# Reordering the projections of a hybrid encoder's even layer on one core: spatial value groups ahead of the heads' output gates

## The chip, the cores and the metric

The kernel runs on one core of one Trainium2 chip. The metric is the device time of one execution in microseconds (us), less is better. The core has five engines with instruction queues of their own, each worked off in order: TensorE (PE, with its weight loads shown apart as PEld), VectorE (DVE), ScalarE (ACT), GpSimd (POOL) and SyncE (SP, which issues most of the transfers).

## The reference, cut to what matters

Two layers over 1024 tokens of width 1024, float32. The change lies in the even layer's mixer:

```python
p = rms_norm(x) @ w_in                       # 24 blocks of 128 columns, plus 16 gate columns
qk, va, oa, gates, uv = split(p)             # q: blocks 0-3, k: 4-7, v: 8-11, oa: 12-15, u: 16-19, vb: 20-23
qk = silu(centred_dwconv(qk, conv_w))        # 5 taps
ha = rms_norm(h_fwd + h_bwd, head_g) * sigmoid(oa)      # 4 heads of a chunkwise mLSTM, both directions
u, vb = split(gelu(uv)); vb = rms_norm(vb)   # 4 groups
hb = u * (ws @ vb + bs)                      # in chunks of 128 tokens
x = x + concat([ha, hb]) @ w_out
```

After it come a squared-ReLU MLP, an attention layer, a second MLP and a final norm, none of which the change touches.

## The kernel before

Every weight block of 128x1024 is loaded on SP's queue (`raw`), rounded on ACT (line 411, `whi`) and its rest taken on POOL (line 412, `wlo`). A projection multiplies it with the normalized input in three passes (hi x hi, hi x lo, lo x hi): 48 matmuls of 128x512 into a PSUM tile `mm` of which there are two (line 432). DVE scales it on its way out of PSUM into a tile `pt` (`evac`, line 990). `AB_ORDER` is the order in which the blocks are loaded; the calls of `k_unit`, `q_unit`, `v_unit`, `o_unit`, `vb_unit` and `u_unit` must come in the same order.

What follows a projection:

- `k_unit`, `q_unit`: the convolution (ACT line 997, four DVE operations of line 1001, ACT Silu line 1003).
- `v_unit`, then `v_turn`: eight transposes of v (tile `vT`, line 1029) and two ACT copies.
- `o_unit`: an ACT Sigmoid (line 1036).
- `vb_unit`: an ACT Gelu (line 1047). `turn(g)` calls `sgu_values`: eight transposes (`vbT`, line 1424), ACT copies to `vn` (line 1426), and `tok_norm`. `mix(g)` calls `sgu_mix`: eight small products with `ws` (tile `sp`, line 1439, 16 matmul records) and two DVE operations (line 1440).
- `u_unit`: an ACT Gelu (line 1057) and a product with the group's `sp` on POOL (on DVE for the last group, line 1059).

Each head is a generator (`mlstm`), advanced by `step(h)`. Its five parts are: (1) the scores S (line 1277), the transposes kT (line 1286), their weighting on DVE, the decay matrices Dm from DRAM, masked on POOL and put through Exp on ACT; (2) the chunk states U (line 1304), with a chain of DVE operations (line 1313); (3) the products `int` and `intra` (lines 1339 and 1350), their sum, division (lines 1362 to 1371) and the sum of both directions on POOL (line 1385); (4) `tok_norm`; (5) eight transposes `hT` (line 1396) and two DVE products with the sigmoid of the output gate (line 1399).

`tok_norm` is an ACT square, a DVE reduction (line 1411), a chain of twelve DVE operations on 128x8 elements (lines 1413 and 477 to 486), each of which waits for the one before it, and a full-size product (line 1415).

All the small PE work takes its PSUM from one pool:

```python
pp = st.enter_context(tc.tile_pool(name="pab", bufs=4, space=PSUM, reuse_waits="tile"))
def sm(name="sm"):
    return pp.tile([P, 512], F32, tag="sm", name=self.uid(name))
```

SBUF tiles come from a ring of 45 slots, handed out in the order in which they were given back. In this stage no order is written out by hand: a planner lays the instructions of each engine out with priorities by the order of the program and estimated times, and hands its slots and tiles out in that order; the result is a fixed in-order list per engine. After `u_unit(3)` come the output projections (`mlp_inputs`, line 885), which read the eight tiles split by `add` (ACT line 501, POOL or DVE line 502), and the first MLP.

Of the kernel before, what the change touches and what calls it, by code (L numbers as in the profile page):

```python
# [76 lines left out]

AB_ORDER = (4, 0, 8, 5, 1, 9, 12, 6, 2, 10, 13, 7, 3, 11, 14, 15, 20, 21, 22, 23, 16, 17, 18, 19)  # L80

C_ORDER = (0, 1, 5, 2, 3, 4)

# [226 lines left out]
class Kern:  # L310
# [55 lines left out]
    def plan(self):  # L366
        A = self.A
        self.sd = [[self.dp.tile([4, P, 1024], F32, name=f"sd{i}_{j}") for j in range(NKP)] for i in range(2)]
        w = [(A["w_g"], NK * 48, True)]
        w += [(A["w_in"][i], 1024) for i in AB_ORDER]  # L370
        w += [(A["ab_out"][m], 1024) for m in MO]
# [572 lines left out]
    def ab(self, xh, xl, ss, spill):  # L944
# [37 lines left out]
        def evac(ps):  # L982
            t = self.slot(name="pt")
            with self.tc.high_priority():
                if isinstance(ps, list):
                    for h in range(2):
                        hs = slice(h * 512, (h + 1) * 512)
                        nc.vector.tensor_tensor(out=t[:, hs], in0=ps[h], in1=rb[:, hs], op=ALU.mult)
                else:
                    nc.vector.tensor_tensor(out=t, in0=ps, in1=rb, op=ALU.mult)  # L990
            return t
# [19 lines left out]
        def k_unit(h, ps=None):  # L1011
            R[h]["k"] = conv(4 + h, ps)

        def q_unit(h, ps=None):
            R[h]["q"] = conv(h, ps)

        def v_unit(h):
            R[h]["vt"] = evac(self.proj(xh, xl))

        def v_turn(h):  # L1020
            vt = R[h].pop("vt")
            v = R[h]["v"] = self.slot(F32, (P, NC, 130), "v")
            nc.gpsimd.memset(v[:, :, P:P + 1], 1.0)
            nc.gpsimd.memset(v[:, :, P + 1:P + 2], 0.0)
            for g in range(2):
                ps = sm("vT")
                for j in range(4):
                    c = 4 * g + j
                    nc.tensor.transpose(ps[:, j * P:(j + 1) * P], vt[:, c * P:(c + 1) * P], self.ident)
                with self.tc.high_priority():  # L1030
                    nc.scalar.copy(out=v[:, 4 * g:4 * g + 4, :P], in_=ps.rearrange("p (j e) -> p j e", e=P))
            self.drop(vt)

        def o_unit(h):
            oa = evac(self.proj(xh, xl))
            nc.scalar.activation(oa, oa, AF.Sigmoid)
            R[h]["oa"] = oa
# [3 lines left out]
        def vb_unit(g):  # L1041
            if g == 0:
                sg["ws"] = self.slot(name="ws")
                nc.sync.dma_start(out=sg["ws"][:, :512], in_=A["wsT"])
                nc.sync.dma_start(out=sg["ws"][:, 512:1024], in_=A["bs"].partition_broadcast(P))
            vb = evac(self.proj(xh, xl))
            nc.scalar.activation(vb, vb, AF.Gelu_apprx_tanh)
            sg[g] = vb

        def turn(g):  # L1050
            sg[g] = self.sgu_values(sg[g])

        def u_unit(g):
            u = evac(self.proj(xh, xl))
            if g == 3:
                self.drop(*xh, *xl)
            nc.scalar.activation(u, u, AF.Gelu_apprx_tanh)
            sp = sg.pop(g)
            (nc.vector if g == 3 else nc.gpsimd).tensor_tensor(out=sp, in0=sp, in1=u, op=ALU.mult)
            self.drop(u)  # L1060
            return sp

        def mix(g):
            sg[g] = self.sgu_mix(g, sg[g], sg["ws"][:, :512], sg["ws"][:, 512:])

        def step(h):
            next(G[h], None)
# [5 lines left out]
        for h in range(AH - 1):  # L1073
            k_unit(h + 1)
            if h > 0:
                step(h - 1)
            v_turn(h)
            step(h)
            q_unit(h + 1)
            step(h)  # L1080
            v_unit(h + 1)
            step(h)
            o_unit(h)
            step(h)
        o_unit(3)
        step(2)
        v_turn(3)
        step(3)
        vb_unit(0)
        step(3)  # L1090
        vb_unit(1)
        step(3)
        turn(0)
        vb_unit(2)
        step(3)
        turn(1)
        mix(0)
        vb_unit(3)
        step(3)
        turn(2)  # L1100
        mix(1)
        self.rope_tables()
        ah, al = [], []

        def add(t, **kw):
            hi, lo = self.split(t, **kw)
            ah.append(hi)
            al.append(lo)
            self.drop(t)
        late = []  # L1110
        for g in range(4):
            late.append(u_unit(g))
            if g == 0:
                turn(3)
                mix(2)
            if g == 1:
                mix(3)
                for h in range(AH):
                    add(R[h]["out"], pool=True)
            if g > 1:  # L1120
                add(late[g - 2], pool=True)
# [810 lines left out]
```

## Time and profile before

| | us |
|---|---|
| median of three runs | 2484.16 (2482.21 to 2487.2) |
| the profiled execution, its own time | 2484.26 |
| its span, first to last instruction | 2482.6 |

The span is 1.66 us shorter than the execution's own time. A time slice of the profile gives busy time of each engine in it; PEclk is the granted clock of TensorE as a share of 2.4 GHz. "idle before <-X" is the time for which the engine stood still ahead of an instruction, and whose end let it go.

### The profile page before, as it was taken

How to read it: one execution, taken by the hardware profiler on the slowest of the kernel's cores; microseconds unless marked ns; L12 is line 12 of the kernel's file. 1: busy time of each engine (PE TensorE's matmuls, PEld its weight loads, DVE VectorE, ACT ScalarE, POOL GpSimd, SP SyncE). 2: the span in 40 equal slices, each digit the busy share in tenths (PEclk: the TensorE clock that was granted, in tenths of full speed). 3: DMA queues.
4: the chain of work that ended last, by engine and by line, in shares of the span. 5: the costliest groups of instructions: out<-in, count | busy, mean ns of one | idle time of the engine just before them, and what ended most of it. 6: DMA issues, size and time to landing. Idle time of an engine off the chain costs nothing.

```text
span 2482.6 us, 31418 instructions
## 1 busy us (share of the span) xinstructions
PE 2405.1 (97%) x11947; PEld 1999.9 (81%) x11947; DVE 1773.4 (71%) x2504; ACT 1159.5 (47%) x1717; POOL 576.3 (23%) x362
## 2 busy tenths in 40 slices
PE   7999989999999999999999999998999999999997
PEld 5788877778887788887788888887878888788887
DVE  6765487777777676664788888887577777667665
ACT  3354444433333333353567677677443333333353
POOL 4233344200000000024545454546310000000023
PEclk9999999999999999999999999999999999999999
DMA  3211113365568634351000000002346655953432
GB/s 116 69 60 63 49 48 115 139 229 203 217 221 298 213 110 153 108 172 39 22 18 22 18 19 17 13 26 94 119 146 235 226 207 215 341 162 97 160 109 96
DMA packets 96631, 309.49 MB, mean 125 GB/s; under 512 B 9984, under 2 KB 12992, under 8 KB 96480
## 3 DMA queue, kind: packets, MB, share of 16 engines
q1 hardware_dynamic: 95296, 304.81, 35.1%
q10 hardware_dynamic: 1152, 2.62, 0.3%
q8 instruction: 94, 1.54, 0.3%
q14 instruction: 57, 0.47, 0.1%
q0 software_dynamic: 32, 0.05, 0.0%
HBM read 219.53 MB, written 87.92 MB: 124 GB/s over the span
## 4 chain that ended last, share of the span: by engine, by line
PE 87%; DVE 7%; DMA 3%; ACT 1%; issue 1%; POOL 1%; DVEq 0%; ACTq 0%; POOLq 0%; SPq 0%
PE mm L432 18%; PE y L792 11%; PE z L792 11%; PE A L655 7%; PE C L655 6%; PE D L655 6%; PE s L1680 6%; PE po L1733 4%; PE pt L1714 4%; PE pj L432 4%; PE B L655 3%; DMA raw<-w 1%; DVE mx L1684 1%; DMA hq<-hd 1%; DVE nm L1686 1%
## 5 line engine op out<-in xcount | busy, mean ns | idle before, releaser
L411 ACT CAST whi<-raw 128x1024 fp32r<-128x1024 f32 x163 | 169.2, 1038 | 453.1 <-issue 226.5
L412 DVE TENSOR_TENSOR wlo<-raw,whi 128x1024 fp32r<-128x1024 f32 x110 | 138.6, 1260 | 208.9 <-ACT whi L411 204.8
L432 PE MATMUL mm<-hi,wlo 128*128 128x512 f32 x680 | 218.1, 399 | 2.6 <-POOL wlo L412 2.5
L432 PE MATMUL mm<-hi,whi 128*128 128x512 f32 x680 | 218.4, 399 | 0.0
L432 PE MATMUL mm<-lo,whi 128*128 128x512 f32 x680 | 218.3, 399 | 0.0
L1699 POOL TENSOR_SCALAR pr<-pr,rs 128x1024 f32<-128x1024 f32 x128 | 144.4, 1128 | 242.7 <-DVE rs L1698 203.2
L655 PE MATMUL A<-xo,wo 128*128 128x512 f32 x768 | 190.8, 397 | 1.4 <-DVE x L885 1.4
L655 PE MATMUL D<-xo,wo 128*128 128x512 f32 x768 | 188.8, 394 | 0.0
L1684 DVE TENSOR_REDUCE mx<-s 128x1 f32<-128x1024 f32 x128 | 155.6, 1216 | 46.5 <-PE s L1680 45.8
L655 PE MATMUL C<-xo,wo 128*128 128x512 f32 x768 | 188.6, 394 | 0.0
L412 POOL TENSOR_TENSOR wlo<-raw,whi 128x1024 fp32r<-128x1024 f32 (+1 forms) x53 | 131.2, 2477 | 244.4 <-ACT whi L411 208.1
L792 PE MATMUL y<-hi,wlo 128*128 128x512 f32 (+1 forms) x464 | 180.7, 389 | 2.5 <-DVE wlo L412 2.5
L792 PE MATMUL y<-hi,whi 128*128 128x512 f32 (+1 forms) x464 | 180.8, 390 | 0.0
L1692 ACT ACTIVATE pr<-s,nm,rqs 128x1024 f32<-128x1024 f32 x128 | 154.7, 1209 | 55.1 <-DVE nm L1686 53.2
L792 PE MATMUL y<-lo,whi 128*128 128x512 f32 (+1 forms) x464 | 180.3, 389 | 0.0
L655 PEld LDWEIGHTS A<-xo,wo 128*128 128x128 f32 x768 | 146.1, 191 | 35.5 <-issue 1.8
L1716 ACT CAST pth<-pt 128x512 fp32r<-128x512 f32 x256 | 138.2, 589 | 77.2 <-PE pt L1714 76.6
L655 PEld LDWEIGHTS D<-xo,wo 128*128 128x128 f32 x768 | 144.3, 188 | 33.9
L655 PEld LDWEIGHTS C<-xo,wo 128*128 128x128 f32 x768 | 144.0, 188 | 34.0 <-issue 0.4
L1718 DVE TENSOR_TENSOR ptl<-pt,pth 128x512 fp32r<-128x512 f32 x256 | 163.7, 680 | 7.1 <-ACT pth L1716 6.2
L792 PE MATMUL z<-hi,whi 128*128 128x512 f32 (+1 forms) x400 | 155.9, 390 | 0.0
L792 PE MATMUL z<-hi,wlo 128*128 128x512 f32 (+1 forms) x400 | 155.1, 388 | 0.5 <-DVE wlo L412 0.5
(352 smaller groups left out, 5511.1 us busy)
## 6 DMA issues: line engine op xcount, KB each, us to landing
raw<-w SPq DMA_DIRECT2D x112, 512.0 KB, 4.3
w2q<-w SPq DMA_DIRECT2D x64, 512.0 KB, 5.2
sd<-w2q SPq DMA_DIRECT2D x64, 512.0 KB, 6.6
hd<-c SPq DMA_DIRECT2D x64, 512.0 KB, 2.9
hq<-hd SPq DMA_DIRECT2D x64, 512.0 KB, 4.6
raw<-sd SPq DMA_DIRECT2D x64, 512.0 KB, 3.6
raw<-w_in SPq DMA_DIRECT2D x24, 512.0 KB, 3.6
xs<-x SPq DMA_DIRECT2D x24, 512.0 KB, 3.2
```

Of the source, the lines that this page charges most:

```text
L411: nc.scalar.copy(out=hi[:, :cols], in_=raw[:, :cols])
L412: self.lo_engine.tensor_tensor(out=lo[:, :cols], in0=raw[:, :cols], in1=f(hi[:, :cols]), op=ALU.subtract)
L432: nc.tensor.matmul(ps[:m, o:o + c], lhsT=w, rhs=x[:, t:t + c], start=k == first and i == 0, stop=k == (n - 1 if last is None else last) an ...
L655: nc.tensor.matmul(ps, lhsT=a, rhs=x, start=first and kk == 0 and j == 0, stop=last and kk == NK // 2 - 1 and j == 2, skip_group_check=not ...
L792: nc.tensor.matmul(Z[z, p][:, :c], lhsT=l[:, m], rhs=r[:, k], start=new and kp == 0 and kk == 0 and j == 0, stop=kp == NKP - 1 and kk == 1 ...
L1680: nc.tensor.matmul(ps[:, hsl], lhsT=lhs[:, qs], rhs=rhs[:, hsl], start=a, stop=z)
L1684: nc.vector.reduce_max(out=mx, in_=ps, axis=AX.X)
L1692: nc.scalar.activation(pr, ps, AF.Exp, bias=nm, scale=r["qs"][:, qb:qb + 1], accum_out=su)
L1699: nc.gpsimd.tensor_scalar(out=pr, in0=pr, scalar1=rs, scalar2=1.0, op0=ALU.mult, op1=ALU.mult)
L1714: nc.tensor.transpose(pt[:, j * P:(j + 1) * P], pr[:, c * P:(c + 1) * P], self.ident)
L1716: nc.scalar.copy(out=pth[half][:, :, qo], in_=pvs[half])
L1718: nc.vector.tensor_tensor(out=ptl[half][:, :, qo], in0=pv, in1=f(pth[half][:, :, qo]), op=ALU.subtract)
```

## The change

The number and kind of all instructions stay the same; blocks 12 to 15 (output gates) and 20 to 23 (spatial values) trade places in the order. In the loop over the heads a spatial value group is projected where an output gate was. The group's transposes and norm (`turn`) come where the head's last part (`step`, fifth call) was, and its product (`mix`) one projection later. Behind the loop come the last value group, the four output gates with the heads' last parts between them, and the remaining parts of head 3.

```diff
-AB_ORDER = (4, 0, 8, 5, 1, 9, 12, 6, 2, 10, 13, 7, 3, 11, 14, 15, 20, 21, 22, 23, 16, 17, 18, 19)
+AB_ORDER = (4, 0, 8, 5, 1, 9, 20, 6, 2, 10, 21, 7, 3, 11, 22, 23, 12, 13, 14, 15, 16, 17, 18, 19)
@@
             k_unit(h + 1)
             if h > 0:
-                step(h - 1)
+                turn(h - 1)
             v_turn(h)
             step(h)
             q_unit(h + 1)
             step(h)
+            if h > 0:
+                mix(h - 1)
             v_unit(h + 1)
             step(h)
-            o_unit(h)
+            vb_unit(h)
             step(h)
-        o_unit(3)
-        step(2)
+        vb_unit(3)
+        turn(2)
         v_turn(3)
         step(3)
-        vb_unit(0)
+        o_unit(0)
         step(3)
-        vb_unit(1)
+        mix(2)
+        o_unit(1)
+        turn(3)
+        step(0)
         step(3)
-        turn(0)
-        vb_unit(2)
+        o_unit(2)
+        step(1)
         step(3)
-        turn(1)
-        mix(0)
-        vb_unit(3)
-        step(3)
-        turn(2)
-        mix(1)
+        o_unit(3)
+        mix(3)
+        step(2)
         self.rope_tables()
@@
             late.append(u_unit(g))
             if g == 0:
-                turn(3)
-                mix(2)
+                step(3)
             if g == 1:
-                mix(3)
                 for h in range(AH):
                     add(R[h]["out"], pool=True)
```

## Rows read from the trace of the kernel before

**Rows 1.** The page: busy time and share of each engine, and the chain of work that ended last.

```profile
PE 2405.1 (97%) x11947; PEld 1999.9 (81%) x11947; DVE 1773.4 (71%) x2504; ACT 1159.5 (47%) x1717; POOL 576.3 (23%) x362
PE 87%; DVE 7%; DMA 3%; ACT 1%; issue 1%; POOL 1%; DVEq 0%; ACTq 0%; POOLq 0%; SPq 0%
```

**Rows 2.** Busy time by stretch: from and to, length, then PE, PEld, DVE, ACT, POOL with their instruction counts, the granted clock, the share of the DMA engines and GB/s. The cuts stand at head 0's v transposes, those of heads 1, 2 and 3, the end of head 3's third part, the last small product, and the end of the output projections.

```profile
128.00:182.00 54.00, 54.00 (x299) 46.36 (x298) 32.51 (x55) 30.00 (x64) 18.15 (x12) 1.00 0.17 59
182.00:239.00 57.00, 57.00 (x318) 49.12 (x316) 35.49 (x57) 27.95 (x56) 18.53 (x11) 1.00 0.20 65
239.00:294.00 55.00, 55.00 (x306) 47.44 (x305) 25.85 (x50) 25.11 (x53) 18.91 (x9) 1.00 0.17 58
294.00:326.00 32.00, 32.00 (x201) 28.40 (x200) 13.08 (x27) 11.95 (x29) 9.48 (x4) 1.00 0.11 35
326.00:395.00 69.00, 57.82 (x287) 49.08 (x286) 61.78 (x115) 26.67 (x33) 33.38 (x14) 0.90 0.17 58
395.00:474.00 79.00, 79.00 (x343) 63.96 (x342) 54.10 (x54) 36.82 (x48) 30.88 (x13) 1.00 0.36 127
```

**Rows 3.** PE in order of time around its three waits: start, length, line, operation, tiles, count, and in brackets the idle time before with what ended it.

```profile
350.49 3.27 PE L1439 MATMUL sp<-ws,vn 128*128 128x128 f32 x16 [2.74 <-DVE vn L1415]
357.97 1.97 PE L1396 MATMUL hT<-ident,hd 128*128 128x128 f32 x8 [4.21 <-DVE hd L1415]
359.59 1.20 PE L432 MATMUL mm<-hi,wlo 128*128 128x512 f32 x2
360.59 0.96 PE L432 MATMUL mm<-hi,whi 128*128 128x512 f32 x2
...
383.11 3.76 PE L1439 MATMUL sp<-ws,vn 128*128 128x128 f32 x16 [4.24 <-DVE vn L1415]
386.52 1.20 PE L432 MATMUL mm<-lo,whi 128*128 128x512 f32 x2
387.52 1.05 PE L432 MATMUL mm<-hi,wlo 128*128 128x512 f32 x2
388.37 0.74 PE L432 MATMUL mm<-hi,whi 128*128 128x512 f32 x2
388.96 0.63 PE L432 MATMUL mm<-lo,whi 128*128 128x512 f32 x2
```

**Rows 4.** The same kinds of PE work away from the waits: the last products `intra` of heads 0, 1 and 2, the transposes hT and vT that follow them, the transposes of value group 2 and a product sp.

```profile
164.61 0.61 PE L1350 MATMUL intra<-v,Dm 128*128 128x130 f32 x4
181.85 1.04 PE L1396 MATMUL hT<-ident,hd 128*128 128x128 f32 x8
220.15 0.61 PE L1350 MATMUL intra<-v,Dm 128*128 128x130 f32 x4
238.50 1.03 PE L1396 MATMUL hT<-ident,hd 128*128 128x128 f32 x8
275.29 0.61 PE L1350 MATMUL intra<-v,Dm 128*128 128x130 f32 x4
293.88 1.03 PE L1396 MATMUL hT<-ident,hd 128*128 128x128 f32 x8
294.75 1.04 PE L1029 MATMUL vT<-ident,pt 128*128 128x128 f32 x8
368.71 1.95 PE L1439 MATMUL sp<-ws,vn 128*128 128x128 f32 x16
370.49 1.04 PE L1424 MATMUL vbT<-ident,pt 128*128 128x128 f32 x8
```

**Rows 5.** DVE in order of time: the last operation of the norm of heads 0, 1 and 2 (line 1415), and the evacuation of v for head 3 (line 990).

```profile
175.48 1.23 DVE L1415 TENSOR_TENSOR hd<-hd,try 128x1024 f32<-128x1024 f32 x1
214.47 1.23 DVE L990 TENSOR_TENSOR pt<-mm,rb 128x1024 f32<-128x1024 f32 x1 [0.46 <-PE mm L432]
233.60 1.23 DVE L1415 TENSOR_TENSOR hd<-hd,try 128x1024 f32<-128x1024 f32 x1
289.93 1.23 DVE L1415 TENSOR_TENSOR hd<-hd,try 128x1024 f32<-128x1024 f32 x1
```

**Rows 6.** DVE operations grouped by line in the stretch 326 to 395 us: count, busy us, mean ns of one.

```profile
L483 DVE SCALAR_TENSOR_TENSOR trw<-try 128x8 f32<-128x8 f32 x15 | 11.2, 749 | 0.3
L1415 DVE TENSOR_TENSOR vn<-vn,try 128x1024 f32<-128x1024 f32 x4 | 6.2, 1562 | 0.1
L1411 DVE TENSOR_REDUCE tn<-sq 128x8 f32<-128x1024 f32 x5 | 6.1, 1211 | 1.6 <-ACT sq L1409 1.6
L1440 DVE SCALAR_TENSOR_TENSOR sp<-sp,cst,ws 128x512 f32<-128x512 f32 x8 | 5.9, 745 | 3.5 <-PE sp L1439 3.4
```

**Rows 7.** The same for the stretch 182 to 239 us, with the norm of one head in it.

```profile
L1413 DVE TENSOR_SCALAR tn<-tn 128x8 f32<-128x8 f32 x1 | 2.0, 2009 | 0.0
L483 DVE SCALAR_TENSOR_TENSOR trw<-try 128x8 f32<-128x8 f32 x3 | 0.5, 167 | 0.1
```

**Rows 8.** One POOL operation and the DVE operations inside it, in order of time.

```profile
344.08 2.61 POOL L412 TENSOR_TENSOR wlo<-raw,whi 128x1024 fp32r<-128x1024 f32 x1
344.33 2.38 DVE L483 SCALAR_TENSOR_TENSOR trw<-try 128x8 f32<-128x8 f32 x1
```

**Rows 9.** An early wait of PE for a weight, and a load of an activation table on ACT.

```profile
65.07 0.73 PE L432 MATMUL mm<-hi,wlo 128*128 128x512 f32 x2 [2.53 <-POOL wlo L412]
261.10 1.28 ACT L1047 ACT_TABLE_LOAD   x1
```

## The prediction, on record before the changed kernel was run

> **What bounds the kernel now.** I read the page first: PE is busy for 97% of the span, and the chain that ended last runs on PE for 87% of its length and on DVE for 7% [rows 1]. So the time is PE's work plus the places where PE stands still, and a change that leaves the work alone can only move those places. I looked for them next, in the busy time by stretch. From 128 to 326 us PE is busy in every microsecond. From 326 to 395 us it is busy for 57.82 of 69, at a mean granted clock of 0.90; from 395 on it is dense again [rows 2]. In that one stretch DVE is busy for 61.78 us of 69, against 107 of 198 us (54%) in the four stretches ahead of it, and POOL for 33.38 (48%, against 33%).
>
> Then the order of time. PE waits three times there: 2.74, 4.21 and 4.24 us, each for the last operation of a `tok_norm` on DVE (line 1415), twice for a value group, once for head 3 [rows 3]. All three sum to 11.19 us, which is the whole gap between 69 and 57.82. PE works its list off in order, so the projection behind a waiting `sp` product stands too, though it needs nothing from DVE.
>
> The clock falls with each wait. Sixteen `sp` matmuls take 3.27 and 3.76 us right behind a wait and 1.95 us elsewhere; eight `hT` take 1.97 against 1.03; pairs of projection matmuls 1.20, 0.96, 1.20, 1.05 and 0.74 against 0.63 [rows 3, 4]. The small matmuls at about half speed are the level of 1.2 GHz, the others 2.4 GHz. The excess: 1.32 + 1.81 + 0.94 + (0.57 + 0.33 + 0.57 + 0.42 + 0.11) = 6.07 us. So the three waits cost 11.19 + 6.07 = 17.26 us, or 5.75 each.
>
> **Why DVE is late there.** Two causes. First, work is piled up: the four value groups' norms and products, head 3's norm and the rotary tables all fall into this stretch. Second, the chain is slowed: line 483, 8 elements wide, takes 167 ns in the stretch around head 1's norm and 749 ns here [rows 6, 7]. Its 15 instances alone lose 15 x 0.58 = 8.7 us. The single case shows how: POOL's weight operation runs from 344.08 to 346.69, DVE's line 483 from 344.33 to 346.71 [rows 8]; it ends when POOL ends. The Trainium skill's page "SBUF — State Buffer", section "Who interferes with whom", says that a DVE operation with two SBUF inputs fully blocks against a GpSimd operation that reads SBUF. These rows agree; the page gives the mechanism of the slower rival below.
>
> **The change, part by part.** PE: the same 24 projections and the same small products, so 0 us of work. What counts is the order of the small ones. Their PSUM tiles come from one pool of four in program order. The trace shows the effect: v of head 3 is evacuated at 214.47 [rows 5], but its transposes vT start only at 294.75, in direct succession to `hT` of head 2 at 293.88 [rows 4]. Every head so waits for the norm of the one before. From the last `intra` of a head to the next `hT`: 181.85 - 165.22 = 16.6, 238.50 - 220.76 = 17.7, 293.88 - 275.90 = 18.0 us [rows 4]. After the change the fifth part is no longer in that place; a value group's `turn` is, whose projection is long done. So the three heads behind the first come 52 us earlier in sum, less the added small work (three `vbT` of 1.04 and two `sp` of 1.95, 7 us [rows 4]): head 3's vT at some 250 us instead of 295, an estimate.
>
> The tail: of the four `turn` and `mix` pairs none is left behind the last `u` projections; only head 3's `hT` and the rotary tables are. The norm for each lies at least a projection ahead of its use. The three waits of [rows 3] have then no instruction of their kind left in front of the last projections: -17.26 us.
>
> The middle: DVE gets four value norms and products and head 3's norm earlier. One norm is 1.21 for the reduction, 12 x 0.17 for the chain and 1.23 for the product, about 5 us with the gaps where POOL isn't in the way, a `mix` 2 x 0.745, some 1.4 us of DVE [rows 5 to 7]; so 4 x 6.4 + 5 = 31 us on top of 107 us, in some 190 us: 73% instead of 54%, an estimate that stays below the 90% of the tail. PE doesn't wait for a norm in the middle now, and there is slack: head 0, 1 and 2's `hT` start 181.85 - 176.71 = 5.1, 238.50 - 234.83 = 3.7 and 293.88 - 291.16 = 2.7 us after their norm's end [rows 4, 5]. A norm there that meets one POOL operation loses 2.01 - 0.17 = 1.84 us [rows 7], less than the least slack. The price of too little slack is 5.75 us for each wait. Between none and three I take half a wait, +2.9 us, since a norm that meets two POOL operations (3.7 us) would pass two of the three slacks; bounds 0 and three waits (17.26).
>
> Output gates: a head's `hT` holds its PSUM tiles until DVE's product with the sigmoid, which needs that gate's projection. Head 0's `hT` now stands ahead of head 3's third part in the pool. If the gate is late, PE still has projections in its list; 0 us, cover being those projections, and without it one wait of 5.75.
>
> DMA: the two loads for `ws` (256 KB each) move on SP's queue from behind the last gate's weight to ahead of the second value weight or so; the weight loads queued behind them feed ACT, POOL, then PE. The nearest row is the one wait of PE for a weight, 2.53 us [rows 9]; I take 0 because two weights are buffered, and keep 2.53 as the bound. ACT: Gelu comes in the loop, between other functions, where Sigmoid was; one load more or less of a table is 1.28 us [rows 9] on an engine that is busy for 95 of 198 us [rows 2]: 0, hidden by that idle time. SBUF: heads' sums, `ws` and products live longer; counting the takes and returns of slots in the code, the ring's least number free falls from 13 to 11 in this stage. Still eight or more program steps between return and reuse: 0.
>
> Sum: 2484.26 - 17.26 + 2.9 = 2469.9, so 2470 us. The profiled execution is 0.1 us above the median, so nothing has to be shifted. The changes behind the stage (MLP, attention) are none: 0.
>
> **The rivals.**
> (a) Forecast: the tail runs dense, at most one wait stays: 2484.26 - 17.26 = 2467 to 2473. For it: every wait of PE in the stage after 66 us is in the tail. Chance 0.60.
> (b) Some waits come back in the middle, one and a half to two and a half: 2473 to 2482, with two 2478.5. For it: DVE at 73% and POOL operations between the norm's steps. Chance 0.20.
> (c) The waits only move: three remain, behind the output gates or at head 3's last part, which is still placed among the `u` projections, next to the rotary tables: 2484, within 5 us. Against it: the pile of [rows 2] is spread over heads. Chance 0.10.
> (d) Slower, through POOL and DVE excluding each other in the middle. Eight norms now lie between 165 and 315 us, where POOL has its Dm, sum and weight operations of 2.4 us; with heads some 40 us apart they collide more often. It decides from more than three of the eight norms stalling PE (17.26 / 5.75). With five: 2484.26 - 17.26 + 28.75 = 2495.8. Against it: the three norms that lie there now stall none. By the skill's rule alone, in which the second to come always blocks, this is the outcome if POOL comes first each time; the three rows above speak for less. Chance 0.10.
>
> **How the numbers follow.** The predicted time is (a)'s, 2470. A measurement of this kernel tells 0.2%, about 5 us. Faster by more than that holds in all of (a) and three quarters of (b): 0.60 + 0.15 = 0.75. Same: the rest of (b) and (c), 0.15. Slower: (d), 0.10. The range runs from (a) without any wait, less 3 us for the spread of the runs and bubbles at clock edges, to the end of (b): 2464 to 2482, with 0.80 and a little of (c) inside; (a)'s own range is 2464 to 2473.
>
> **What would show it.** In the profile after: PE's `vT` of heads 1 to 3 right behind `vbT`, not behind `hT`, head 3's near 250 us; the last `sp` product ahead of the first `u` evacuation; PE busy throughout from 300 us to the output projections and a granted clock near 1.00 there; the output projections' end 14 us earlier. DVE's line 483 mean well below 749 ns in the last 70 us of the stage. The prediction is wrong if PE shows waits for line 1415 between 165 and 315 us, if the heads keep their distance of 56 us, or if a gate's or weight's wait stands where the norm's stood.

## The result, and the profile after

The changed kernel takes 2463.54 us (median of five runs, 2461.64 to 2472.72) against 2482.21 us before in the same series: a ratio of 0.9932, 95% interval 0.9918 to 0.9947, so 16.9 us less, with 13.2 as the least and 20.4 as the most of the interval. The forecast was 2470 us, 14.3 below the profiled execution of before. The median itself lies half a microsecond under the stated range of 2464 to 2482; but the kernel before was quicker in this series too, and the ratio, taken on the 2484.26 us that the forecast started from, gives 2467.4. The profiled execution after took 2467.47 us with a span of 2465.7, which is 16.9 us less than the span before.

First the stretches of [rows 2], at the same times, after:

```profile
128.00:182.00 54.00, 54.00 (x320) 46.95 (x319) 36.76 (x55) 36.17 (x78) 25.28 (x15) 1.00 0.17 56
182.00:239.00 57.00, 57.00 (x336) 49.63 (x335) 45.65 (x106) 29.20 (x62) 17.59 (x11) 1.00 0.16 56
239.00:294.00 55.00, 55.00 (x324) 47.88 (x323) 31.85 (x67) 28.55 (x57) 17.44 (x8) 1.00 0.14 48
294.00:326.00 32.00, 32.00 (x186) 27.56 (x185) 26.11 (x60) 15.54 (x31) 11.84 (x5) 1.00 0.10 29
326.00:395.00 69.00, 69.00 (x314) 56.37 (x313) 22.59 (x31) 22.71 (x23) 33.70 (x15) 1.00 0.29 99
```

PE is busy throughout, the granted clock is 1.00 in all five, and the last stretch holds 314 PE records where it held 287. POOL is as busy there as before (33.70 against 33.38 us), but DVE has 22.59 us of work beside it where it had 61.78. The DVE work has gone to the stretches ahead, most of it to the second to fourth.

Then PE in order of time, where [rows 4] showed `vT` behind `hT`:

```profile
171.45 1.03 PE L1029 MATMUL vT<-ident,pt 128*128 128x128 f32 x8
...
194.76 1.95 PE L1439 MATMUL sp<-ws,vn 128*128 128x128 f32 x16
...
262.28 1.03 PE L1424 MATMUL vbT<-ident,pt 128*128 128x128 f32 x8
263.15 0.60 PE L1029 MATMUL vT<-ident,pt 128*128 128x128 f32 x4
...
325.32 1.95 PE L1439 MATMUL sp<-ws,vn 128*128 128x128 f32 x16
327.10 1.04 PE L1396 MATMUL hT<-ident,hd 128*128 128x128 f32 x8
339.13 1.03 PE L1396 MATMUL hT<-ident,hd 128*128 128x128 f32 x8
```

Head 3's v transposes stand behind the value group's, at 263 us instead of 295. The last value product is done at 327 us; behind 340 us no small product is left, only projections. From head 0's v transposes to the first MLP no PE row carries a wait any more.

To take the change's own part out of one execution I cut it at two instructions that both kernels have, head 0's first v transpose and the first product of the first MLP. Before, then after:

```profile
128.35 1.03 PE L1029 MATMUL vT<-ident,pt 128*128 128x128 f32 x8
473.64 2.24 PE L655 MATMUL A<-xo,wo 128*128 128x512 f32 x9
```

```profile
132.33 1.04 PE L1029 MATMUL vT<-ident,pt 128*128 128x128 f32 x8
462.23 2.26 PE L655 MATMUL A<-xo,wo 128*128 128x512 f32 x9
```

Between them lie 345.3 us before and 329.9 us after. That is 15.4 us less; call this stretch the mixer. Its busy times, before and then after (columns as in [rows 2]):

```profile
128.35:473.64 345.29, 334.11 (x1737) 283.82 (x1736) 222.16 (x356) 158.50 (x280) 128.97 (x61) 0.98 0.21 73
132.33:462.23 329.90, 329.90 (x1740) 279.53 (x1739) 208.09 (x357) 161.07 (x282) 128.56 (x61) 1.00 0.21 73
```

DVE is busy for 14 us less with the same work; the section on POOL's operations below shows why. The start is 4.0 us longer in this profile, and what comes behind is 5.5 us shorter. Whether these two belong to the change is a question for the runs below.

### The profile page after: what moved, and what is told of

It is laid out like the page before. It is cut to its first block, busy times and chain, and to the rows that moved or that the text cites. A ratio compares the mean times of both kernels' runs of the same rounds, so it can differ in the third digit from the quotient of the medians.

```text
span 2465.7 us, 31388 instructions
## 1 busy us (share of the span) xinstructions
PE 2401.5 (97%) x11947; PEld 1993.5 (81%) x11947; DVE 1753.1 (71%) x2504; ACT 1161.5 (47%) x1718; POOL 574.0 (23%) x362
## 4 chain that ended last, share of the span: by engine, by line
PE 88%; DVE 5%; issue 2%; DMA 2%; POOL 1%; ACT 1%; DVEq 0%; SPq 0%; ACTq 0%; POOLq 0%
PE mm L432 18%; PE y L792 12%; PE z L792 11%; PE A L655 7%; PE C L655 7%; PE D L655 7%; PE s L1680 6%; PE po L1733 4%; PE pt L1714 4%; PE pj L432 4%; PE B L655 4%; DVE mx L1684 1%; DMA raw<-w 1%; POOL x L289 1%; PE mm L448 1%
## 5 line engine op out<-in xcount | busy, mean ns | idle before, releaser
L412 POOL TENSOR_TENSOR wlo<-raw,whi 128x1024 fp32r<-128x1024 f32 (+1 forms) x53 | 131.5, 2482 | 245.9 <-ACT whi L411 216.0
```

The source lines that it names most:

```text
L412: self.lo_engine.tensor_tensor(out=lo[:, :cols], in0=raw[:, :cols], in1=f(hi[:, :cols]), op=ALU.subtract)
```

## The experiments

Two theories were on the table for the mixer's 15.4 us: (A) the order in the PSUM pool, by which heads waited for each other's norms; (B) the pile of DVE work in the tail, slowed by POOL. All times of one series share their runs of the kernel before. "The mixer" is the stretch just defined, from each run's own trace.

| run | ratio to before, 95% interval | mixer, us | PE's waits in it, us |
|---|---|---|---|
| before | 1 | 345.3 | 11.2 |
| the change | 0.9932 (0.9918 to 0.9947) | 329.9 | 0 |
| e1_gates_late | 0.9962 (0.9950 to 0.9975) | 339.3 | 6.9 |
| e2_values_early | 1.0002 (0.9993 to 1.0011) | 343.5 | 10.2 |
| e3_rests_on_dve | 0.9934 (0.9919 to 0.9949) | 332.8 | 3.4 |
| e4_tables_early | 0.9982 (0.9973 to 0.9991) | 338.3 | 6.7 |
| e5_before_no_value_norm | 0.9956 (0.9938 to 0.9973) | 333.4 | 3.4 |
| e6_after_no_value_norm | 0.9967 (0.9954 to 0.9980) | 332.9 | 1.8 |
| e8_after_rests_on_dve | 0.9941 (0.9926 to 0.9956) | 329.9 | 0 |
| e7_after_two_waits | 0.9914 (0.9899 to 0.9929) | 333.7 | 3.8 |
| e9_after_spread_late | 0.9901 (0.9886 to 0.9916) | 329.9 | 0 |
| e10_after_again | 0.9944 (0.9932 to 0.9957) | 329.9 | 0 |

### Half the change: the heads' last parts out of the loop

```diff
         for h in range(AH - 1):
             k_unit(h + 1)
-            if h > 0:
-                step(h - 1)
             v_turn(h)
...
-        step(2)
         v_turn(3)
         step(3)
         vb_unit(0)
         step(3)
         vb_unit(1)
+        step(0)
         step(3)
         turn(0)
         vb_unit(2)
+        step(1)
         step(3)
         turn(1)
         mix(0)
         vb_unit(3)
+        step(2)
         step(3)
```

> The kernel before with its order of projections kept (output gates ahead of the value groups); only the fifth part of heads 0 to 2 is taken out of the loop and comes after the value groups 1, 2 and 3. Theory A (the order of the small PE work in the one PSUM pool is the lever: each head's v transposes stood behind the transposes of the head before, and so behind its norm): head 3's v transposes move from 295 us to 240 to 260, the value groups find a DVE that has no head's work left beside them, PE idles under 5 us between 150 us and the first MLP, and the time falls by 10 to 17 us. Theory B (the value groups' norms and products piled up behind the last projections are the cause, wherever the heads are): the heads come earlier too, but the four value norms still lie among the u projections; at least 8 us of waits for line 1415 stay and the time falls by less than 5 us.

The heads did come earlier: head 3's `vT` starts at 252.25 us. The gain is 9.4 us by the ratio, 6.0 us in the mixer, and these PE waits are left there (who waited for whom, us, times, longest):

```profile
PE sp L1439 <- DVE vn L1415: 3.4, 2, 3.2
PE hT L1396 <- DVE try L479: 3.1, 1, 3.1
PE intra L1350 <- ACT C L1308: 0.3, 1, 0.3
```

Both theories miss: the pool's order does set when the heads come, as A has it, but freeing them removes only 4.3 of 11.2 us of waits. The value norms still lie in the tail, as B has it, and keep 3.4 us; another 3.1 stand before the transposes of the last head, behind its own norm.

### The other half: value groups early, heads' last parts in place

```diff
-AB_ORDER = (4, 0, 8, 5, 1, 9, 12, 6, 2, 10, 13, 7, 3, 11, 14, 15, 20, 21, 22, 23, 16, 17, 18, 19)
+AB_ORDER = (4, 0, 8, 5, 1, 9, 20, 12, 6, 2, 10, 21, 13, 7, 3, 11, 22, 14, 23, 15, 16, 17, 18, 19)
             if h > 0:
+                turn(h - 1)
                 step(h - 1)
...
             step(h)
+            if h > 0:
+                mix(h - 1)
             v_unit(h + 1)
             step(h)
+            vb_unit(h)
             o_unit(h)
```

> The opposite half: value groups early as in the changed kernel, but each head's fifth part stays in the loop ahead of the next head's v transposes, as before; for that the output gates are projected in the loop too, behind the value groups. Theory A: the heads keep a distance of 55 to 60 us (with the value work between them rather more), head 3's v transposes stay at 295 us or later, head 3's norm and its transposes fall among the u projections and PE waits there for 4 to 12 us; the gain is under 8 us. Theory B: the value norms are out of the tail, so the gain is that of the whole change, 14 to 18 us, however late head 3 is.

No gain at all. The heads' v transposes start at 129.1, 187.7, 252.4 and 310.0 us, 58 to 65 us apart, since each head now waits for the norm of the last head and for a value product too. Head 3 then falls among the `u` projections (the lines of this kernel are three lower than those above: its line 1393 is line 1396 there):

```profile
PE hT L1393 <- DVE hd L1412: 7.0, 1, 7.0
PE int L1336 <- DVE sp L1437: 2.0, 1, 2.0
PE int L1336 <- DVE num L1359: 1.1, 1, 1.1
```

This is what A expected. Taking norms out of the tail is worth nothing as long as head 3's chain slides into it. The halves give 6.0 and 1.8 us in the mixer, together less than the whole: it needs both, or something else that stands behind both.

### What slows DVE in the tail: POOL's operations moved

```diff
-                    add(R[h]["out"], pool=True)
+                    add(R[h]["out"])
...
-                add(late[g - 2], pool=True)
+                add(late[g - 2])
-        add(late[2], pool=True)
+        add(late[2])
```

> The kernel before; the rests of the mixer's output tiles (line 502, seven operations of 2.4 us on POOL) go to DVE (1.23 us each). If DVE's steps of 8 elements are slow in the tail because POOL's two-input operations shut them out, then 17 us less of POOL work weigh more than 8.6 us more on DVE: line 483 has a mean below 450 ns (749 before), the waits of PE shrink from 11.2 to under 8 us, and the time falls by 3 to 8 us. If DVE's sheer load is the cause, 8.6 us more on an engine that is busy for 90% make the waits longer: 14 to 20 us, and the time rises by 3 to 9 us.

This one edit to the kernel before gives nearly the whole gain, 12.5 us in the mixer, with every projection where it was. The first theory had the sign and the mean of line 483; its size, 3 to 8 us, was too small. In the stretch 326 to 395 us PE waits for 3.4 us:

```profile
326.00:395.00 69.00, 65.60 (x336) 53.84 (x335) 62.95 (x126) 30.59 (x37) 19.88 (x9) 1.00 0.22 72
```

```profile
L502 DVE TENSOR_TENSOR lo<-hT,hi 128x1024 fp32r<-128x1024 f32 x4 | 4.8, 1212 | 0.0
L502 DVE TENSOR_TENSOR lo<-sp,hi 128x1024 fp32r<-128x1024 f32 x4 | 4.8, 1222 | 0.0
L483 DVE SCALAR_TENSOR_TENSOR trw<-try 128x8 f32<-128x8 f32 x15 | 4.6, 306 | 0.3
```

Since this kernel is further along at 395 us than the one before, the fair comparison is the whole mixer:

```profile
127.21:460.05 332.84, 329.44 (x1738) 278.76 (x1737) 217.52 (x363) 158.30 (x280) 111.94 (x54) 1.00 0.22 75
```

DVE took over seven rests of 1.22 us, 8.5 us of work (the eighth was on DVE before), and yet is busy for 4.6 us less than the 222.16 us of before: the shut-out time went with POOL's operations. Two of those collisions in the trace of before, each a POOL operation and the DVE operation beside it:

```profile
336.53 2.47 POOL L502 TENSOR_TENSOR lo<-hT,hi 128x1024 fp32r<-128x1024 f32 x1 [3.45 <-ACT hi L501]
336.63 2.38 DVE L483 SCALAR_TENSOR_TENSOR trw<-try 128x8 f32<-128x8 f32 x1
369.70 2.41 POOL L502 TENSOR_TENSOR lo<-sp,hi 128x1024 fp32r<-128x1024 f32 x1 [4.05 <-DVE tn L1411]
369.80 2.34 DVE L477 TENSOR_SCALAR tri<-tn 128x8 int32<-128x8 int32 x1
```

So the tail's waits come from a collision of two things, the chains of small DVE operations and POOL's operations; they shrink to 3.4 us or less when the seven rests, or the value norms, are taken out of it. The Trainium skill's page "SBUF — State Buffer", section "Who interferes with whom", has the rule for it: a DVE operation with two SBUF inputs and a GpSimd operation that reads SBUF exclude each other. The trace agrees: in the mixer before, 15 of DVE's operations with 128x8 elements in and out last over 0.4 us where the others take some 0.17, and each of the 15 ends 19 to 34 ns after a POOL operation ends. Five of them (lines 1413, 477 and 479) read a single SBUF input, which that sentence isn't about.

What these long operations take beyond 0.17 us each can be summed from the last `intra` to the first MLP. It is 20.6 us before (10.9 by the rests, 6.5 by the weight operations of line 412, 3.2 by the products of line 1059), 10.0 here with the rests' share gone, 6.6 without the value norms (e5) and 2.0 after the change; PE's waits in the mixer of these four are 11.2, 3.4, 3.4 and 0 us.

### How much is DVE's load as such

```diff
             o_unit(h)
             step(h)
+            if h == 1:
+                self.rope_tables()
...
-        self.rope_tables()
         ah, al = [], []
```

> The kernel before; only the rotary tables (some 28 DVE operations of 128x128, 7.6 us in the trace, not read before the attention layer) are made in the loop, behind head 1, instead of in the tail. If the tail's DVE load as such sets the waits, each us taken out of it shortens them: 11.2 us fall to some 4 to 8 us, the time falls by 4 to 9 us. If what counts is only the chain of the norms in the pool's order, the tables fill DVE's gaps and taking them away changes less than 2 us of waits and the time by less than 3 us.

The waits fall to 6.7 us and the mixer by 7.0, as the first theory says; the ratio's 4.5 us lies at its lower end. DVE in the stretch 326 to 395 us has 54.05 us instead of 61.78. That isn't load alone: the long operations of the tail, summed as above, lose 15.1 us here instead of 20.6. The edit took load and collisions out together, and this run doesn't part them.

### The value norms left out, before and after

In both kernels `sgu_values` ends without its `tok_norm`:

```diff
         self.drop(vb)
-        self.tok_norm(vn)
         return vn
```

> The kernel before without the norm of the value groups (the kernel leaves out the square, the sum, the reciprocal root and the product for the four groups; heads keep theirs): four of the five norms in the tail are gone. If the four value norms are what PE waits for, the waits for value products (6.98 us) vanish, head 3's shrinks, PE idles under 3 us in the stage, and the time falls by 12 to 18 us. If the tail is bound by the pool's order and head 3 alone, the wait of head 3's transposes (4.2 us) stays and the gain is under 8 us.

> The changed kernel with the same left out (norm of the four value groups). If the changed order hides these norms altogether, the time is that of the changed kernel, 2460 to 2467 us. If they still cost something in the middle that the trace doesn't show as a wait (the sp products ahead of the heads' int products hold the pool), it falls by 4 us or more below that, and the heads come closer together than 46 us.

Before, it takes 11.9 us off the mixer, and of the three waits one is left, head 3's, 3.4 us. So the value norms were the larger part of the pile, and the wait of head 3 stays with its own norm. The waits for value products vanish, as the first theory says, but it is missed in size: 3.4 us of waits where it had under 3, and 10.9 us by the ratio where it had 12 to 18.

After, both theories fail: with less work the ratio is 6 to 9 us above that of the changed kernel (0.9944 and 0.9932 in its two series), and the mixer takes 3.0 us longer. New PE waits show in the middle:

```profile
PE int L1339 <- DVE C L1313: 1.0, 1, 1.0
PE U L1304 <- DVE kw L1291: 0.7, 1, 0.7
```

The planner laid the middle out anew: head 2's v transposes come 38 us behind head 1's instead of 43, head 3's then 55 us behind instead of 49, and the two waits stand in head 2's `U` and `int`, at 219 and 232 us. So leaving the value norms out brings the changed kernel nothing, but as the plan differs too, the run can't say what they cost in the plan of the changed kernel. That the tighter place of head 2 is the reason for the waits is argued from the two rows, not shown.

### Both cures at once

```diff
 # on the changed kernel
-                    add(R[h]["out"], pool=True)
+                    add(R[h]["out"])
...
```

> The changed kernel with the seven rests of the mixer's output on DVE as well, the edit that alone gave the kernel before 15 us. If both edits remove the same waits (the collisions of POOL and DVE in the tail), there is nothing left to gain: within 3 us of the changed kernel, 2460 to 2467 us. If they act on different things, the gains add up: 2448 to 2455 us.

The mixer takes 329.9 us, to a tenth the changed kernel's. The two edits remove the same waits; nothing adds up. (The 15 us in the expectation are e3's whole time; in the mixer its gain was 12.5.) The time itself, 14.7 us below before, is within the change's interval.

### The same cure elsewhere

```diff
 # on the changed kernel, in strassen_up
-                if g == 6:
+                if g == 7:
                     rb[0] = self.spread_sums(dg, NC, True, [bank("B"), bank("C")])
 # and in ab / run
-        self.lo_engine = nc.gpsimd
         spill = [[...
         q_unit(0, q0)
+        self.lo_engine = nc.gpsimd
```

> The changed kernel with the same cure at two other waits of PE: the products that spread the norm over PSUM in both MLPs (wait for line 561's tile, 3.5 us in the first and as much again in the second, each followed by a slow stretch) come one product later, and the first two weight rests of the mixer are taken on DVE instead of POOL (wait of 2.4 us at 65 us). If PE's waits with the slow clock behind them cost what the trace shows (two times 5 to 6 us and one time 3 to 4), the time falls by 8 to 15 us below the changed kernel, to 2449 to 2456 us. If DVE is just as late one product on, or the slow clock costs nothing of its own, it falls by less than 5 us.

The first half worked in both MLPs. The wait at 486.90 us in the changed kernel, and the same place in this run:

```profile
480.81 2.94 PE L655 MATMUL D<-xo,wo 128*128 128x512 f32 x12
486.90 0.49 PE L574 MATMUL B<-dg,ones_r 128*128 128x512 f32 x1 [3.15 <-DVE dg L561]
489.48 3.59 PE L655 MATMUL A<-xo,wo 128*128 128x512 f32 x12
```

```profile
484.16 2.94 PE L655 MATMUL A<-xo,wo 128*128 128x512 f32 x12
487.46 0.49 PE L574 MATMUL B<-dg,ones_r 128*128 128x512 f32 x1 [0.36 <-DVE dg L561]
489.39 2.94 PE L655 MATMUL C<-xo,wo 128*128 128x512 f32 x12
```

The second half removed the wait at 65 us, but the planner then laid the mixer out anew and four waits of 0.3 to 1.6 us came up in it, 3.8 us in all. The time was 21.4 us below before, 4.5 more than the change by the ratios: under the 8 to 15 of the first theory, and the number of the second, though not for its reasons, since the waits that the edit was aimed at did shrink. So the first half was run alone:

> The changed kernel with only the first half of the edit before it: the products that spread the norm in both MLPs come one product later; the weight rests stay on POOL. The mixer's instructions are then those of the changed kernel. If what the edit before it gave back in the mixer (PE waits of 3.9 us between 200 and 250 us, 3.7 us more from head 0's v transposes to the first MLP) came from the weights on DVE, the mixer takes 330 us again, the two MLPs keep their gain of 3 and 5 us, and the time is 7 to 9 us below the changed kernel's. If the mixer's waits come by themselves from run to run, they are here too.

With the weight rests back on POOL the mixer is 329.9 us again, its PE order that of the changed kernel. The ratio is 0.9901: 24.6 us below before, the fastest of all the kernels here (2457.10 us, 2455.39 to 2460.15). Below the changed kernel that is 7.7 us by the first series' ratio, as expected, and 10.7 by the ratio of the same series (next section).

### What belongs to the change, and what to the execution

> The changed kernel once more, unaltered. In its first profile three stretches differ from the kernel before's: from the start to head 0's v transposes 4.0 us longer, from there to the first MLP 15.4 us shorter, and the attention layer's scores (525.3 us against 530.3) 5 us shorter, although no engine's order differs there. If the last is the change's doing (slots at other places), it shows 525 us again; if it differs from execution to execution of any kernel, 528 to 531 us. The mixer should take 330 us either way, and the start 127 to 132 us.

The mixer took 329.9 us again. The attention layer's first score matmuls ran from and to these times, in before, after, the last experiment and this one:

```profile
L1680 PE MATMUL s<-Kh,hi x256: 387/394/628, 1198.0 to 1728.3; 128*128 128x512 f32 x128
```

```profile
L1680 PE MATMUL s<-Kh,hi x256: 387/393/504, 1185.6 to 1710.9; 128*128 128x512 f32 x128
```

```profile
L1680 PE MATMUL s<-Kh,hi x256: 387/394/796, 1180.1 to 1705.3; 128*128 128x512 f32 x128
```

```profile
L1680 PE MATMUL s<-Kh,hi x256: 387/394/796, 1182.5 to 1712.6; 128*128 128x512 f32 x128
```

That is 530.3, 525.3, 525.2 and 530.1 us: one and the same kernel shows 525 and 530. So the 5 us belong to the execution. The start, too, varies from 127.2 to 132.3 us over these traces. Repeated, the ratio is 0.9944, 13.9 us; the change's own gain is the mixer's 15.4 us, and it lies in both intervals.

## Why the prediction was right, step by step

**The three waits.** Forecast -17.26 us, of it 11.19 idle time and 6.07 for the slow clock behind it. The idle time went to the last tenth. The clock term came out too large: 15.4 - 11.2 leaves 4.2 us. Of the difference, 0.3 us is known: the lengths of matmul rows end at modelled ends, and by starts alone the excess in [rows 3] is 5.8 us. The other 1.6 us stay open: without waits and excess the mixer before has 345.3 - 11.2 - 5.8 = 328.3 us, the one after 329.9, and where the dense work takes longer wasn't found. e3 shows when the term is small: its five waits of 0.3 to 1.1 us came at a granted clock of 1.00, and its mixer less its waits, 332.8 - 3.4 = 329.4, holds no slow stretch.

**The remainder.** +2.9 us for half a wait in the middle; it was 0. So the two errors (1.9 and 2.9) have opposite signs and partly cancel, which is luck: 14.4 forecast met 15.4.

**The cause of DVE's lateness.** Of its two halves, pile and shutting out, the second weighed more than the text had it: e3 cured nearly everything without any reordering and with 8.5 us more work for DVE. How much sheer load adds stays open, since e4 took load and collisions out together. The prediction had the lock from a single pair of rows [rows 8], with a weight operation in it, and didn't see that the seven rests took the largest share in the tail, 10.9 of 20.6 us.

**The pool's order.** Right in kind: `vT` follows `vbT`, and the heads lead. Too bold in size: head 3's `vT` was to be near 250 us and stands at 263; of these 13 us 4 belong to the later start of this execution. The step that failed counted only the added PE work (7 us), while the value product that now precedes `int` in the pool waits for its own norm: in the changed kernel U of head 2 ends by 235 us and `sp` starts at 243.80, behind the norm's end at 240.1. So a value norm seems to take part of the place of the head's norm in the chain. e6 speaks against it as the whole cause: without these norms head 3's `vT` comes 133 us behind head 0's, and with them 131. What holds the heads at that distance stays open. It didn't matter to the time, because projections filled PE. e1 and e2 show that the reordering's gain needs this order but doesn't come from it alone.

**The middle.** DVE was to rise to 73%; from 128 to 326 us it is busy for 140.4 of 198 us, 71%, and for 80% in the fullest stretch. Rival (d) had the mechanism right: the norms do meet POOL there, about once each. But a meeting costs less there than in the old tail. DVE in the changed kernel from 165 to 315 us, with seven norms in it:

```profile
L483 DVE SCALAR_TENSOR_TENSOR trw<-try 128x8 f32<-128x8 f32 x21 | 4.6, 220 | 0.4
L1413 DVE TENSOR_SCALAR tn<-tn 128x8 f32<-128x8 f32 x7 | 4.0, 587 | 0.0
L479 DVE TENSOR_SCALAR try<-tri 128x8 int32<-128x8 int32 x7 | 3.3, 477 | 0.0
L477 DVE TENSOR_SCALAR tri<-tn 128x8 int32<-128x8 int32 x7 | 2.1, 319 | 0.0
```

Against 0.17 us each, these four lose 1.1 + 2.9 + 2.1 + 1.0 = 7.1 us, about 1 us a norm; the five norms in the old tail lost 20.6 us, 4.1 each. e6 and e7 show that the margin was thin all the same: other plans of the same middle have waits of 1.8 and 3.8 us. The plan of the changed kernel had none in four traces (the change, e8, e9 and e10).

**Gates, transfers, tables, slots.** Costed at nothing, and no PE wait for a gate, a weight or a table shows in the mixer after. The wait for a weight at 65 us is there as before, 2.4 us.

## What to carry to other kernels

When an in-order engine waits for a chain of tiny operations on another, look first at what shuts that chain out: moving seven POOL operations to DVE gave 12.5 us in the mixer where the reordering gave 15.4, and both together no more than 15.4. Count such a wait with the slow stretch behind it (here 11.2 us of waits cost 15.4), and put the consumer one independent product later where the producer can't be hurried: that simple edit brought 8 to 11 us in two places. Where a planner lays out the order, each edit moves all the rest, so read the gain from a stretch between two instructions that all kernels share, not from the whole time alone.

## What the runs showed of the hardware that was not expected

- A DVE operation with 128x8 elements in and out took some 0.17 us (0.36 at most), or as long as a POOL operation still had to run: in the mixers of the twelve traces 120 of them lasted over 0.4 us, and every one ended 17 to 36 ns after a POOL operation. The means of line 483 (749, 306, 220 and 167 ns in four stretches) only count how many were hit: 4 of 15, 1 of 15, 1 of 21 and none of 3.
- The attention layer, whose order is the same on every engine in before, after, e8, e9 and e10, took 525 or 530 us between its first and last score matmul, in executions of one kernel too. Its cause wasn't looked for.
